# First norm over pairs of tiles, a shorter 1/rms, modulation in pairs and a split FFN buffer in a two-block transformer kernel

## The chip, the cores and the metric

The kernel runs on one core of one Trainium2 chip. The metric is the device time of one execution in microseconds (us), and lower is better. The engines are named as the profile names them: PE (TensorE, with PEld for its weight loads), DVE (VectorE), ACT (ScalarE), POOL (GpSimd) and SP (SyncE, which here only issues DMAs). SPq and ACTq are rows of DMA issue.

## What is computed

Two transformer blocks follow each other on 512 tokens of width 1024, in fp32. The first is an adaptive-norm block: six shifts, scales and gates come from a condition vector, the mixer is a gated linear attention (GLA) in both directions beside a differential attention over context and tokens, and a SwiGLU FFN follows. The second block has a mixer of windowed pooling and forgetting attention, a cross-attention to 256 memory rows, and an FFN with a width-3 convolution.

```python
def rmsnorm(x, g):  return x * rsqrt(mean(x * x, -1) + EPS) * g
def modulate(x, g, shift, scale):  return rmsnorm(x, g) * (1 + scale) + shift

# first block
sh1, sc1, gt1, sh2, sc2, gt2 = split(silu(c) @ w_mod + b_mod, 6)
px = modulate(x, norm1_g, sh1, sc1) @ w_in           # the context goes the same way: pc
mix = concat([gla_merge(og, r, gla_norm_g), diff_merge(od, diff_norm_g)]) @ w_out
x = x + gt1 * mix
x = x + gt2 * swiglu(modulate(x, norm2_g, sh2, sc2), w_ffn_in, w_ffn_out)
# second block
x = x + rms_norm(merged @ w_mix_out, mix_post_g)
x = x + rms_norm(mem_attention(rms_norm(x, xa_pre_g), rms_norm(mem, mem_g), w_xq, w_xkv, w_xo), xa_post_g)
x = x + rms_norm(conv_ffn(rms_norm(x, ffn_pre_g), w_up, conv_w, conv_b, w_down), ffn_post_g)
```

## The kernel before

**Layout and products.** Activations are held feature-major: eight tiles (KT = 8) of 128 features by 512 tokens (S = 512). Each weight matrix comes from HBM as fp32, in pieces of 512 KB mostly, into a ring of two buffers (tag `wf`), and `wsplit` (L171) cuts each into a high part, cast on ACT (L185), and the low rest, subtracted on DVE or POOL (L186). `mm3` makes each product of three matmuls: high x high, high x low, low x high (L194 to L196, and L283 to L285 where the tokens stand in the rows). PSUM has named slots: `acc`, `s` (from `s1` and `s2`), `mis`, `sums`.

**Order.** The engines' programs are laid out ahead by a scheduler that takes instructions by priority, and each engine then runs its own in order. `tc.issue_after(ins)` keeps an instruction behind another one. SP issues the loads in program order, and a load whose buffer isn't free holds those behind it.

**The start** (L401 to L500). X comes in four loads of two tiles. `normed_x` (L424) squares each tile, the even ones on ACT and the odd ones on DVE, and `sum_sq` (L308) sums over the features by matmuls with a column block of ones, four for a tile. `warm` (L481) issues matmuls on the identity whose results nobody reads: `WU` of them ahead of the first sum, `WX` ahead of each later one, `WW` behind the first modulations. `mod_tiles` and `mod_block` (L342) make the first 16 of 48 modulation tiles, from eight 1 MB loads (`wm`): matmuls with `silc` = silu(c) (L350), a copy out of PSUM (`mr`, L353), and `mod_sums` (L359): transposes (L362), a reduce over the partial sums (L363), the addition of the bias (L365).

**1/rms.** `rsqrt` (L156) makes v = mean + eps (DVE, L162), y = exp(-0.5 ln v) on ACT (L163, L164), and one Newton step in four DVE operations (L165 to L168). The names of its tiles say which norm it is: r_x and r_c (tokens and context in block one), r_n (second norm), r_post and r_pre (the norms of block two). `bcast` (L325) spreads r over the partitions with matmuls (L329).

**The other 32 modulation tiles** come in 32 steps of 512 KB. `mod_step` (L750) loads one piece into the same ring as the weights and runs its matmuls (L762); four steps fill one 512-wide `acc`, which ACT copies to `mr` (L766); `mod_end` (L769) calls `mod_sums` with a slot `s`. Two steps run in each of the first twelve of the 16 GLA units (`MU`, L1023), and `mod_end` in every second unit. The last eight steps are fillers of the attention stage.

**Fillers.** A list of jobs whose matmuls are laid into stages that don't fill PE; `fill_in` and `fill_to` take from it. In the attention stage they are, in order: the remaining gate projections (`gr_jobs`), `mix_in`, eight `mem_in` (load of a memory tile on ACT's queue, split by ACT and DVE, L1162 to L1165), the eight modulation steps, and the memory's keys and values (`mem_k`, `mem_v`). `mem_sq` (L714) squares the memory tiles early, through loads on ACT's queue.

**The output projection and the second norm.** `fm` (L217) runs a product tile by tile; after each quarter of a tile (`every`) it takes one step of whatever generator lies in `between`. `ev_out` (L1296) adds an output tile to X and squares it for the norm; `norm2` (L1304) yields `W4` or `W5` times, makes the statistics, yields, broadcasts and normalises. It is run for the two token halves; the second half's steps lie inside the first products of the FFN.

**The two FFNs** share `ffn_hidden` (L1330). It opens 22 hidden tiles in high and low parts: eight lie in free slots, the rest in the tiles `early`, `Fhi` and `Flo` of the pool that is passed (`fp` or `fp2`). Until the hidden state fills them, parts of `Fhi` and `Flo` take split weights (`room`). The second FFN's pool `fp2` (L1750) is opened when the pools of the cross-attention, `xp` and `xt` (L1658), have been closed (`xa.close`, L1742); it lies in their place. `KV` is the first tile of `xp`, and the last thing done with it is X = X + KV (L1428) of the second token half. In `fp2` stand, in order of allocation, `zl`, `early`, `Fhi`, `Flo`, and then the two buffers of `z`, which POOL first writes with a memset (L1760).

**The end.** `result` (L1789) sums the last squares, runs `rsqrt`, broadcasts (L1800), scales, adds and stores.

## Time and profile before

| | us |
|---|---|
| median of three runs | 1653.22 |
| lowest and highest | 1652.99, 1656.14 |
| the profiled execution | 1654.39 |
| its span, first to last instruction | 1652.6 |
| PE busy in it | 1600.5 (97%) |
| DVE, ACT, POOL busy | 948.7 (57%), 716.8 (43%), 214.1 (13%) |
| mean granted clock of PE | 0.989 |

Busy times are of one execution. A matmul's end is modelled, so a busy PE isn't always PE at its peak, and the rows of neighbouring instructions overlap a little. In a timeline the bracket behind a row tells how long the engine had been idle before it and what released it. The profiled execution's time is its span and 1.8 us around it.

### The profile page before, as it was taken

Reading aid. Unit: us, or ns where it says so; the run is one execution under the profiler, and the core shown is the slowest. Engines: PE = TensorE matmul, PEld = TensorE weight load, DVE = VectorE, ACT = ScalarE, POOL = GpSimd, SP = SyncE. Lnnn points to the kernel's source line nnn. Section 1 sums busy time; section 2 is a strip of 40 time slices with the busy share of each in tenths; the row PEclk is TensorE's granted clock in tenths of the full one; section 3 lists DMA queues with packets and bytes.
Section 4 is the critical chain, followed back from the end, with each engine's and each line's share of the span. In section 5 each row is a group of like instructions: output and inputs, shape, how many; then the busy total and the mean of one; then the engine's idle time right before and its main releaser. Section 6 shows DMA issues by size and latency. Waiting matters only on the chain.

```text
span 1652.6 us, 25497 instructions
## 1 busy us (share of the span) xinstructions
PE 1600.5 (97%) x10146; PEld 1359.2 (82%) x10146; DVE 948.7 (57%) x1799; ACT 716.8 (43%) x1345; POOL 214.1 (13%) x236
## 2 busy tenths in 40 slices
PE   8998999999999999999999999999998999999997
PEld 6898877768999888888889777888988988888887
DVE  5647787868756222223335676445788777776333
ACT  3534445567745323232223565224466544444221
POOL 0400000111012222110004000122000222221001
PEclk9999999999999999999999999999999999999998
DMA  9132245232323333332332212234210223323332
GB/s 373 53 95 81 79 152 160 80 122 74 130 72 109 90 91 101 102 91 89 101 117 71 77 39 64 90 102 146 86 50 27 90 90 102 102 90 96 96 93 74
DMA packets 48903, 162.98 MB, mean 99 GB/s; under 512 B 5648, under 2 KB 11280, under 8 KB 47248
## 3 DMA queue, kind: packets, MB, share of 16 engines
q1 hardware_dynamic: 45040, 157.74, 30.5%
q10 hardware_dynamic: 3456, 3.33, 0.7%
q8 instruction: 80, 1.31, 0.3%
q0 software_dynamic: 288, 0.28, 0.1%
q14 instruction: 39, 0.32, 0.1%
HBM read 158.46 MB, written 3.15 MB: 98 GB/s over the span
## 4 chain that ended last, share of the span: by engine, by line
PE 87%; DVE 6%; ACT 3%; issue 2%; DMA 1%; POOL 1%; ACTq 0%; DVEq 0%; POOLq 0%
PE acc L194 16%; PE acc L195 16%; PE acc L196 16%; PE s L195 5%; PE s L196 5%; PE s L194 5%; PE acc L284 3%; PE acc L283 2%; PE acc L285 2%; PE mis L1135 2%; PE mis L1607 1%; PE acc L762 1%; DVE wlo L186 1%; DMA wm<-in_w_mod 1%; PE s L1106 1%
## 5 line engine op out<-in xcount | busy, mean ns | idle before, releaser
L185 ACT CAST whi<-wf 128x1024 fp32r<-128x1024 f32 (+4 forms) x221 | 228.7, 1035 | 421.1 <-PE acc L195 291.0
L186 DVE TENSOR_TENSOR wlo<-wf,whi 128x1024 fp32r<-128x1024 f32 (+2 forms) x183 | 221.7, 1211 | 176.2 <-ACT whi L185 170.8
L195 PE MATMUL acc<-qlo,whi 128*128 128x512 f32 (+1 forms) x640 | 238.9, 373 | 0.0
L196 PE MATMUL acc<-qhi,wlo 128*128 128x512 f32 (+1 forms) x640 | 238.9, 374 | 0.0
L194 PE MATMUL acc<-qhi,whi 128*128 128x512 f32 (+1 forms) x640 | 238.6, 373 | 0.0
L194 PEld LDWEIGHTS acc<-qhi,whi 128*128 128x128 f32 x640 | 120.7, 189 | 19.7
L195 PEld LDWEIGHTS acc<-qlo,whi 128*128 128x128 f32 x640 | 120.6, 189 | 19.6 <-issue 0.2
L196 PEld LDWEIGHTS acc<-qhi,wlo 128*128 128x128 f32 x640 | 120.7, 189 | 19.4
L195 PE MATMUL s<-qlo,whi 128*128 128x512 f32 (+1 forms) x336 | 127.4, 379 | 0.0
L194 PE MATMUL s<-qhi,whi 128*128 128x512 f32 (+1 forms) x336 | 127.4, 379 | 0.0
L196 PE MATMUL s<-qhi,wlo 128*128 128x512 f32 (+1 forms) x336 | 127.4, 379 | 0.0
L186 POOL TENSOR_TENSOR wlo<-wf,whi 128x1024 fp32r<-128x1024 f32 x38 | 90.9, 2393 | 213.5 <-ACT whi L185 213.5
L1392 DVE TENSOR_TENSOR e<-e,s 128x512 f32<-128x512 f32 (+1 forms) x22 | 14.3, 652 | 154.0 <-PE s L196 153.8
L195 PE MATMUL acc<-glo,whi 128*128 128x512 f32 (+1 forms) x208 | 74.5, 358 | 0.1
L196 PE MATMUL acc<-ghi,wlo 128*128 128x512 f32 (+1 forms) x208 | 74.2, 357 | 0.0
L194 PE MATMUL acc<-ghi,whi 128*128 128x512 f32 (+1 forms) x208 | 74.2, 357 | 0.0
L194 PEld LDWEIGHTS s<-qhi,whi 128*128 128x128 f32 x336 | 63.2, 188 | 11.9
L196 PEld LDWEIGHTS s<-qhi,wlo 128*128 128x128 f32 x336 | 63.2, 188 | 11.9
L195 PEld LDWEIGHTS s<-qlo,whi 128*128 128x128 f32 x336 | 63.2, 188 | 11.6
L194 PE MATMUL acc<-Fhi,whi 128*128 128x512 f32 (+1 forms) x187 | 71.5, 383 | 0.0
L196 PE MATMUL acc<-Fhi,wlo 128*128 128x512 f32 (+1 forms) x187 | 71.5, 383 | 0.0
L195 PE MATMUL acc<-Flo,whi 128*128 128x512 f32 (+1 forms) x187 | 71.5, 382 | 0.0
(648 smaller groups left out, 3832.0 us busy)
## 6 DMA issues: line engine op xcount, KB each, us to landing
wf<-in_w_ffn_in SPq DMA_DIRECT2D x44, 512.0 KB, 3.6
wf<-in_w_up SPq DMA_DIRECT2D x44, 512.0 KB, 3.5
wm<-in_w_mod SPq DMA_DIRECT2D x32, 512.0 KB, 4.1
wm<-in_w_mod SPq DMA_DIRECT2D x8, 1024.0 KB, 13.1
wf<-in_w_ffn_out SPq DMA_DIRECT2D x16, 512.0 KB, 3.6
wf<-in_w_g SPq DMA_DIRECT2D x16, 512.0 KB, 3.5
wf<-in_w_down SPq DMA_DIRECT2D x16, 512.0 KB, 3.5
wf<-in_w_dv SPq DMA_DIRECT2D x8, 512.0 KB, 4.2
```

The source lines that it names most:

```text
L185: A.copy(hi[:, :n], wf[:, :n])
L186: (lo_eng or V).tensor_tensor(lo[:, :n], wf[:, :n], f32(hi[:, :n]), ALU.subtract)
L194: T.matmul(o, lhi, rhi, start=start, stop=False)
L195: T.matmul(o, lhi, rlo, start=False, stop=False)
L196: ins = T.matmul(o, llo, rhi, start=False, stop=stop).ins
L283: T.matmul(o, bhi(k), whi, start=k == 0, stop=False)
L284: T.matmul(o, bhi(k), wlo, start=False, stop=False)
L285: T.matmul(o, blo(k), whi, start=False, stop=k == KT - 1)
L762: T.matmul(p[32 * j:32 * j + 32, 256 * h:256 * h + 256], silc[:, 4 * kc + j], wf[:, j * 256:(j + 1) * 256], start=kc == 0, stop=kc == 1, s ...
L1106: T.matmul(s_[:, n0:n1], QF[:, c, ts], KA[:, c, n0:n1], start=True, stop=False)
L1135: T.matmul(p[:, :128], aT[:, kt * 128:(kt + 1) * 128], v, start=kt == 0, stop=kt == NKT - 1)
L1607: T.matmul(pO[:, ts], vz[:, kt, hp_, 64 * e:64 * e + 128], pT[:, kt * 128:(kt + 1) * 128], start=kt + e == 0, stop=kt - t + e == 1, skip_g ...
```

## The change

It has seven parts.
- **First norm.** Tiles are squared in pairs, one on ACT and one on DVE, and DVE adds the two squares; `sum_sq` runs once a pair. `WU` goes from 12 to 15 and `WX` from 2 to 1. The load of `cols` (biases, gains) moves from ACT's queue to SP's, behind X. The first modulation tiles are tied behind the last sum.
- **1/rms.** Ln reads its source itself, with the scale and a bias tile `epsc`; v is still made, beside it. Three operations follow instead of four.
- **Modulation in pairs.** `mod_step` fills 256 columns in two steps, and `mod_end` handles two tiles, once in each GLA unit. In the attention stage a pair of steps with its end stands behind each of the last two gate projections and the first two `mem_k`, instead of four and four behind `mem_in`.
- **Memory squares.** Their loads wait for the last activation of the context's modulation.
- **Output projection.** The first evictions are issued first and their squares after them.
- **Second norm.** `W4` goes from 2 to 1, and three yields instead of one stand between statistics and broadcast in the second half.
- **FFN buffer.** The high part is split into `Fend` (four tiles, allocated first) and `Fhi`; `early` is allocated last of these, `zl` at its first use. `room` has three entries instead of five, of which six in all (three of them None) are drawn.

```diff
-WU, WX, WW = 12, 2, 5
+WU, WX, WW = 15, 1, 5
-W4, W5 = 2, 1
+W4, W5 = 1, 1
...
+    epsc = const.tile([128, 1], F32, name="epsc")
+    nc.gpsimd.memset(epsc, EPS)
...
+        A.activation(y, src, AF.Ln, scale=scale, bias=epsc)
         V.tensor_scalar(v, src, scale, EPS, ALU.mult, ALU.add)
-        A.activation(y, v, AF.Ln)
         last_rs[0] = A.activation(y, y, AF.Exp, scale=-0.5).ins
-        V.tensor_tensor(t, y, y, ALU.mult)
-        V.tensor_tensor(t, t, v, ALU.mult)
-        V.tensor_scalar(t, t, -0.5, 1.5, ALU.mult, ALU.add)
-        V.tensor_tensor(r, y, t, ALU.mult)
+        V.scalar_tensor_tensor(t, v, -0.5, y, ALU.mult, ALU.mult)
+        V.tensor_tensor(t, t, y, ALU.mult)
+        V.scalar_tensor_tensor(r, t, 1.5, y, ALU.add, ALU.mult)
...
-        nc.scalar.dma_start(cols, a["cols"])
+        nc.sync.dma_start(cols, a["cols"])
...
-            for k in range(KT):
-                t = st2.tile([128, S], F32, tag=f"sqt{k % 2}", name="sqt")
-                if k % 2:
-                    V.tensor_tensor(t, x[:, k], x[:, k], ALU.mult)
-                else:
-                    A.activation(t, x[:, k], AF.Square)
+            for k in range(0, KT, 2):
+                t, u = (st2.tile([128, S], F32, tag=f"sqt{j}", name="sqt") for j in range(2))
+                A.activation(t, x[:, k], AF.Square)
+                V.tensor_tensor(u, x[:, k + 1], x[:, k + 1], ALU.mult)
+                V.tensor_tensor(u, u, t, ALU.add)
                 with tc.issue_after(warm(WU if k == 0 else WX)):
-                    sum_sq(pt, t, k == 0, k == KT - 1)
+                    last_warm[0] = sum_sq(pt, u, k == 0, k == KT - 2)
+            yield
...
-        mod_tiles(8)
-        next(nx)
-        im = mod_tiles(0)
+        queued(last_warm[0], lambda: mod_tiles(8))
+        ins = next(nx)
+        im = queued(ins, lambda: mod_tiles(0))
+        with tc.issue_after(ins):
+            next(nx)
...
-        nc.scalar.dma_start(m, a["memT"][:, k])
+        with tc.issue_after(hi_at[0]):
+            nc.scalar.dma_start(m, a["memT"][:, k])
...
-        if h == 1 and kc == 1:
-            mr = mid2.tile([128, 512], F32, tag="mr", name="mr")
-            A.copy(mr, p)
+        if kc == 1:
+            mr = mid2.tile([128, 256], F32, tag="mr", name="mr")
+            A.copy(mr, p[:, :256])
...
-        n = mod_at[0] // 4 - 1
+        n = mod_at[0] // 2 - 1
...
-            mod_sums(16 + 4 * n, 4, mr, s2)
+            mod_sums(16 + 2 * n, 2, mr, s2)
...
-        if u % 2 == 0:
-            mod_end()
+        mod_end()
...
+    mods_left = [[(0.8, mod_step), (0.8, mod_step), (0.3, mod_end)] for _ in range(MU, 16)]
     for m in range(GR, 4):
...
         fillers.append(gr_jobs[m])
+        fillers += mods_here()
     fillers.append((0.0, mix_in))
     for k in range(KT):
         fillers.append((0.0, lambda k=k: mem_in(k)))
-    for n in range(MU // 2, 8):
-        fillers += [(0.8, mod_step) for _ in range(4)] + [(0.6, mod_end)]
     for m in range(4):
...
         fillers.append((1.45, lambda m=m: mem_k(m)))
+        fillers += mods_here()
...
         r = fm_stats(sp, sqs[:, x:y], "n2")
-        yield
+        for _ in range(3 if x else 1):
+            yield
         bcast(rb[:, x:y], r)
...
         for m, (p, _, _) in enumerate(parts):
-            ev_out(m, 0, S, p)
+            V.scalar_tensor_tensor(X[m], p, mods[:, 16 + m, 0:1], X[m], ALU.mult, ALU.add)
+        for m in range(len(parts)):
+            add_sq(X[m], m, 0, S)
...
-        early = fp.tile([128, NP, 2, S // 2], F32, tag="Fh2", name="early")
+        NT = FT - KT - NP
+        last = fp.tile([128, 4, S], F32R, name="Fend")
         rest = []
         for n in ("Fhi", "Flo"):
-            t = fp.tile([128, FT - KT - NP, S], F32R, name=n)
+            t = fp.tile([128, NT if rest else NT - 4, S], F32R, name=n)
...
+        F[0] += [last[:, k] for k in range(4)]
+        early = fp.tile([128, NP, 2, S // 2], F32, tag="Fh2", name="early")
+        room = [t[:, 2 * j:2 * j + 2].rearrange("p k s -> p (k s)") for t in rest for j in range(3)]
+        room = [None] * 3 + [(room[j], room[3 + j], None) for j in range(3)]
```

## Rows read from the trace of the kernel before

**Rows 1.** The page, busy times: engine, us (share of span), instructions.
```profile
PE 1600.5 (97%) x10146; PEld 1359.2 (82%) x10146; DVE 948.7 (57%) x1799; ACT 716.8 (43%) x1345; POOL 214.1 (13%) x236
```

**Rows 2.** Waits of PE over the span: total us, times, longest us.
```profile
PE acc L762 <- DMA wm<-in_w_mod: 4.4, 4, 1.8
...
PE mis L1800 <- DVE r_post L168: 1.6, 1, 1.6
PE acc L194 <- DVE X L1297: 1.5, 1, 1.5
...
PE mis L329 <- DVE r_n L168: 1.3, 1, 1.3
...
PE acc L194 <- ACT mhi L1164: 0.9, 1, 0.9
...
PE acc L283 <- ACT mr L766: 0.7, 1, 0.7
PE s L362 <- DVE t_og L167: 0.6, 1, 0.6
...
PE mis L329 <- DVE r_x L168: 0.5, 1, 0.5
...
PE mis L329 <- DVE r_c L168: 0.5, 1, 0.5
```

**Rows 3.** Busy time by stretch: length, engines (instructions), granted clock, DMA share, GB/s.
```profile
25.94:29.35 3.41, 3.41 (x12) 1.84 (x14) 3.41 (x6) 0.00 (x0) 0.00 (x0) 0.50 1.02 384
...
1278.63:1285.46 6.83, 6.22 (x27) 5.92 (x28) 6.07 (x12) 6.59 (x11) 2.03 (x4) 0.50 0.50 148
185.00:335.00 150.00, 139.06 (x1881) 108.83 (x1879) 123.62 (x290) 78.21 (x205) 8.98 (x18) 0.98 0.39 123
```

**Rows 4.** Timeline of the first norm, PE and DVE: start, us, what.
```profile
1.85 4.65 PE L485 MATMUL s<-ident 128*128 128x128 f32 x24 [1.85 <-POOL down L556]
6.34 0.98 PE L311 MATMUL mis<-ones,sqt 128*128 128x32 f32 x8
...
6.44 0.41 DVE L408 TENSOR_TENSOR silc<-cT,silc 128x256 f32<-128x256 f32 x1
...
8.70 0.69 DVE L430 TENSOR_TENSOR sqt<-X 128x512 f32<-128x512 f32 x1 [0.58 <-PE mis L311]
```

**Rows 5.** The first eight modulation loads (`wm`, 0 to 60 us): durations ns, starts.
```profile
L350 PE MATMUL acc<-wm,silc x128: 379/379/569, 16.6 to 48.6; 128*32 128x256 f32 x128
L399 SPq DMA_DIRECT2D wm<-in_w_mod x8: 328/426/737, 3.1 to 26.8; - x8
...
DMA to landing us min/median/max: 7.2/13.1/18.6
```

**Rows 6.** Timeline of the last 1/rms.
```profile
1641.91 0.48 DVE L1787 TENSOR_SCALAR Yd<-acc,cols 128x256 f32<-128x256 f32 x1 [0.93 <-ACT sqt L1786]
...
1642.60 0.16 DVE L162 TENSOR_SCALAR v_post<-mis 128x2 f32<-128x2 f32 x1 [0.20 <-PE mis L311]
1642.79 0.20 ACT L163 ACTIVATE y_post<-v_post 128x2 f32<-128x2 f32 x1 [0.92 <-DVE v_post L162]
1643.02 0.20 ACT L164 ACTIVATE y_post<-y_post 128x2 f32<-128x2 f32 x1
...
1644.16 1.19 PE L1800 MATMUL mis<-ident,r_post 128*128 128x128 f32 x4 [1.60 <-DVE r_post L168]
```

**Rows 7.** Timeline of the second norm's second half.
```profile
500.56 0.60 PE L311 MATMUL mis<-ones,sqs 128*128 128x32 f32 x4 [0.34 <-DVE sqs L1293]
...
504.96 1.23 DVE L186 TENSOR_TENSOR Flo<-wf,Fhi 128x1024 fp32r<-128x1024 f32 x1 [0.21 <-ACT Fhi L185]
```

**Rows 8.** Timeline at the opening of the second FFN: ACT, POOL, PE.
```profile
1277.68 1.05 ACT L185 CAST Fhi<-wf 128x1024 fp32r<-128x1024 f32 x1 [0.97 <-DVE X L1428]
...
1277.84 0.13 POOL L1760 MEMSET z<- 128x2 f32 x2 [131.07 <-DVE X L1428]
...
1278.78 0.58 PE L194 MATMUL s<-qhi,Fhi 128*128 128x256 f32 x1 [4.89 <-ACT Fhi L185]
```

More of the change, by code (lines that the diff above doesn't have):

```diff
@@ L33 @@
 NF = 2
+NWF = 2
 T0 = 1
@@ L173, in wsplit @@
         if wf is None:
-            wf = ring.tile([128, RW], F32, tag="wf", name="wf", bufs=2)
+            wf = ring.tile([128, RW], F32, tag="wf", name="wf", bufs=NWF)
         if shape is None:
@@ L310, in sum_sq @@
         for t in range(sq.shape[-1] // 128):
-            T.matmul(pt[:, 32 * t:32 * t + 32], sq[:, t * 128:(t + 1) * 128], ones, start=start and t == 0, stop=stop,
-                     skip_group_check=True)
+            ins = T.matmul(pt[:, 32 * t:32 * t + 32], sq[:, t * 128:(t + 1) * 128], ones, start=start and t == 0, stop=stop,
+                           skip_group_check=True).ins
+        return ins
     def fm_stats(pool, sq, name):
@@ L750, in mod_step @@
     def mod_step():
-        n, h, kc = mod_at[0] // 4, mod_at[0] // 2 % 2, mod_at[0] % 2
-        if n == 8:
+        n, kc = mod_at[0] // 2, mod_at[0] % 2
+        if n == 16:
             return
         mod_at[0] += 1
-        wf = ring.tile([128, RW], F32, tag="wf", name="wm", bufs=2)[:, :1024]
-        nc.sync.dma_start(wf, a["w_mod"][n, h, kc].rearrange("p k n -> p (k n)"))
-        if h == 0 and kc == 0:
+        wf = ring.tile([128, RW], F32, tag="wf", name="wm", bufs=NWF)[:, :1024]
+        nc.sync.dma_start(wf, a["w_mod"][n // 2, n % 2, kc].rearrange("p k n -> p (k n)"))
+        if kc == 0:
             mod_p["p"] = acc()
@@ L812 @@
     Rq = gp.tile([128, NLEV, 128], BF16, name="Rq")
-    lt0 = ring.tile([128, RW], F32, tag="wf", name="lt0", bufs=2)
+    lt0 = ring.tile([128, RW], F32, tag="wf", name="lt0", bufs=NWF)
     nc.sync.dma_start(lt0[:, :NLEV * 128], a["LT"])
     V.tensor_copy(LT, lt0[:, :NLEV * 128])
-    lt1 = ring.tile([128, RW], F32, tag="wf", name="lt1", bufs=2)
+    lt1 = ring.tile([128, RW], F32, tag="wf", name="lt1", bufs=NWF)
     nc.sync.dma_start(lt1[:, :512], a["Lsm"])
@@ L1220, in out_part, with xk_ahead, mods_here @@
                         lambda p, hi, lo: parts.append((p, hi, lo)), alloc=alloc)
+    def xk_ahead(m):
+        return 0.0, lambda: fm_ahead(a["w_xk"], "xk", m, ML & 1 and G)
+    mods_left = [[(0.8, mod_step), (0.8, mod_step), (0.3, mod_end)] for _ in range(MU, 16)]
+    def mods_here():
+        return mods_left.pop(0) if mods_left else []
     for m in range(GR, 4):
-        fillers += [gr_ahead(m + 1)] if m < 3 else [(0.0, lambda: fm_ahead(a["w_xk"], "xk", 0, ML & 1 and G))]
+        fillers += [gr_ahead(m + 1)] if m < 3 else [xk_ahead(0)]
         fillers.append(gr_jobs[m])
+        fillers += mods_here()
     fillers.append((0.0, mix_in))
@@ L1227 @@
         fillers.append((0.0, lambda k=k: mem_in(k)))
-    for n in range(MU // 2, 8):
-        fillers += [(0.8, mod_step) for _ in range(4)] + [(0.6, mod_end)]
     for m in range(4):
         if m < 3:
-            fillers.append((0.0, lambda m=m: fm_ahead(a["w_xk"], "xk", m + 1, ML & 1 and G)))
+            fillers.append(xk_ahead(m + 1))
         fillers.append((1.45, lambda m=m: mem_k(m)))
+        fillers += mods_here()
     fillers += [(1.45, lambda hf=hf, t=t: mem_v(hf, t)) for hf in range(2) for t in range(2)]
@@ L1332, in ffn_hidden @@
         F = [[sl[:, k] for k in range(KT)] for sl in slot]
-        early = fp.tile([128, NP, 2, S // 2], F32, tag="Fh2", name="early")
+        NT = FT - KT - NP
+        last = fp.tile([128, 4, S], F32R, name="Fend")
         rest = []
         for n in ("Fhi", "Flo"):
-            t = fp.tile([128, FT - KT - NP, S], F32R, name=n)
+            t = fp.tile([128, NT if rest else NT - 4, S], F32R, name=n)
             rest.append(t)
-            F[len(rest) - 1] += [t[:, k] for k in range(FT - KT - NP)]
-        room = [t[:, 2 * j:2 * j + 2].rearrange("p k s -> p (k s)") for t in rest for j in range(5)]
-        room = [None] * 3 + [(room[j], room[5 + j], None) for j in (2, 3, 4, 0, 1)]
+            F[len(rest) - 1] += [t[:, k] for k in range(t.shape[1])]
+        F[0] += [last[:, k] for k in range(4)]
+        early = fp.tile([128, NP, 2, S // 2], F32, tag="Fh2", name="early")
+        room = [t[:, 2 * j:2 * j + 2].rearrange("p k s -> p (k s)") for t in rest for j in range(3)]
+        room = [None] * 3 + [(room[j], room[3 + j], None) for j in range(3)]
         waits = []
@@ L1750 @@
     with tc.tile_pool(name="fp2", bufs=1) as fp:
-        zl = fp.tile([128, 2, 4, 2], F32, name="zl")
+        zl = []
         def pair2(pg_, pu_, i, x, y, held):
             ready(rb_of, x)
+            if not zl:
+                zl.append(fp.tile([128, 2, 4, 2], F32, name="zl"))
             res = []
@@ L1761, in pair2 @@
                 else:
[L1762 removed]
+                    G.tensor_copy(z[:, x:x + 2], zl[0][:, g, i])
                 V.tensor_tensor(z[:, 2 + x:2 + y], p, rb[:, x:y], ALU.mult)
                 if y < S:
[L1765 removed]
+                    G.tensor_copy(zl[0][:, g, i], z[:, y:y + 2])
                 t = fp.tile([128, S], F32, tag=f"zc{g}", name=f"zc{g}", bufs=1)[:, x:y] if held is None else held[:, g]
```

4 lines of the change are left out of this document (1 added, 3 removed).

## The prediction

> **What bounds the kernel now.** I began with the page: TensorE (PE) is busy for 97% of the span [rows 1], so 1652.6 - 1600.5 = 52.1 us of the span have no matmul, and an edit pays only where it shortens one of those holes, or a stretch in which PE's work is itself overhead. Next came the list of PE's waits [rows 2]: each row names what PE stood for, who released it, the total and the longest. The reader should see that it is a long list of short waits, and that the change touches all of the nine rows shown, if most of them little. Then I read the granted clock by stretch [rows 3]: 3.41 us at 0.50, the lower of the two levels (1.2 GHz against 2.4), follow some of these waits, and work at half clock takes twice as long, so such a stretch costs 3.41 / 2 = 1.7 us. Last, the timelines around each edit [rows 4, 6 to 8].
>
> **First norm in pairs.** Before, PE sets this stage: after 24 warm-up passes (12 matmuls of two) from 1.85 on, each of the eight tiles costs 0.98 us of sum passes and two warm-ups, from 6.34 to the first modulation matmul at 16.6 [rows 4, 5], (16.6 - 6.34) / 8 = 1.29 us a tile. DVE has slack: its third square waits 0.58 us for PE to give a tile back [rows 4]. After the change PE has half the sums (four rounds of 0.98) and one warm-up between them, and DVE has a square and an add a pair. An add of two 128x512 tiles isn't in this stage; I take it at the 0.69 of the multiply of the same shape. DVE's first square is over by 6.44. From there: one add 0.69, the condition's multiply 0.41 [rows 4], as much again for two small operations behind it, three pairs of 2 x 0.69 = 4.14: 12.1. Then one round of sums, 0.98: 13.0, against 16.6: **-3.6 us**. The longer first warm-up (30 passes at 4.65 / 24 = 0.19 us, until 7.7) ends about when the first add does, so it hides. The bounds: -4.3 if the seven operations overlap by 0.1 each, as the first square and the multiply behind it seem to; -2.5 if X or `cols` (now behind X on SP's queue) hold DVE for a microsecond.
> Does the gain survive? The loads don't move, so every use comes 3.6 us closer to its landing. PE's list has no wait of this stage's modulation matmuls (L350) for a load; the last of the eight 1 MB loads is issued at 26.8, landings take 7.2 to 18.6 us with a median of 13.1, and the last use is at 48.6 [rows 5]. By the median it lands at 39.9, by the maximum at 45.4; both are before 48.6 - 3.6 = 45.0 or at it. I keep the whole gain, and price its loss as a rival.
>
> **1/rms.** One chain is seen bare at the end [rows 6]: DVE's v starts at 1642.60, Ln at 1642.79, Exp ends at 1643.22, and PE goes on at 1644.16. The change lets Ln start in v's place (0.19 gained, v then lies beside Exp) and makes four DVE operations three: 1644.16 - 1643.22 = 0.94 for four and the hops, about 0.2 each. So -0.39 a chain. v has to come behind Ln, since two readers of one PSUM tile take turns here (L1787 is released by L1786, which only reads the same `acc` [rows 6]), but Exp's 0.20 covers it. PE waits for r_x, r_c, r_n and the last r_post [rows 2]: r_x, r_c and r_post get 0.39 each, r_n is counted below. Three chains before and in the second FFN lie in a row of DVE work, where only the operation saved counts: 3 x 0.2. Sum 3 x 0.39 + 0.6 = **-1.8** (-1.0 with r_x, r_c and r_post alone, each a little short; -2.4 if the other three count in full).
>
> **Modulation in pairs, GLA stage.** Loads, matmuls and the load buffers (`NWF` is 2, as before) stay. Each unit now ends a pair: two copies of 256 columns stand for one of 512, and a turn of the `s` slot with its transposes, reduce and add per unit where it was per two. The slot `acc` comes free after two steps instead of four; PE waits 0.7 us once for that copy [rows 2] and would mostly not, -0.7. Against it stand six more turns of `s`; the one wait on such a turn is 0.6 us [rows 2], once in six. DVE is 123.62 / 150 = 82% busy here [rows 3], so its small extra operations can delay others. I take **-0.7**, the nearest row; bounds -3 (a clock dip goes too) and +4 (each new turn waits 0.6).
>
> **Modulation in the attention stage.** The last eight steps stood in one block behind the memory inputs; now pairs follow the gates and the first two `mem_k`. PE waited 4.4 us in four pieces for these weight loads, the longest, 1.8, in this stage [rows 2]. Spread out, a load has other work to land beside. But the same steps were what PE had to do while ACT split the memory tiles, and PE waits 0.9 for that split already [rows 2]. I take half of the longest wait, **-0.9**; bounds -1.8 - 1.7 = -3.5 with a half-clock stretch gone too, and +2.7 if three more waits of 0.9 come.
>
> **Norm 2, second half.** The statistics come one step earlier, the broadcast keeps its place three steps behind. Now PE waits 0.34 for the squares and 1.3 for r_n, whose last operation queued behind a 1.23-us weight split at 504.96 [rows 2, 7]. A shorter chain passes ahead of that split: -1.3. The squares are no earlier, though: a step is 12 matmuls of 0.12 us, so the 0.34 can become 0.34 + 1.44 = 1.8; I take a third of that, +0.5. **-0.8** (-1.6 to +1.5).
>
> **Small ones.** Evictions of `w_out` before the squares: PE waits 1.5 us for the third eviction [rows 2], which stands behind a weight split on DVE that stays; -0.2 (0 to -1.5). The memory squares' loads leave ACT's queue in the first stage: -0.2 (0 to -0.4).
>
> **FFN buffer in two tiles.** Here is the largest wait, 4.89 us, and 6.83 us at half clock behind it [rows 2, 3, 8]. The split puts a tile where KV was, so that the weight cast (`Fhi`) needn't wait for KV's last reader, X L1428. But rows 8 show that not only ACT's `Fhi` is released by that X: GpSimd's memset of `z`, after 131 us of idleness, is too, 0.16 us later, and `z` is allocated behind Fhi and Flo, far from KV. What all share is not an address but the pool `fp2`, opened when the pools of cross-attention close. If the wait is on the pool, cutting a tile in two changes nothing: **0** (down to -8, below).
>
> **Sum.** -3.6 - 1.8 - 0.7 - 0.9 - 0.8 - 0.4 + 0 = -8.2 us. Against the profiled execution's 1654.39 (span 1652.6 and 1.8 around it) that is 1646.2. The median of the runs shown, 1653.22, lies 1.2 below that execution: 1645.0, which I predict.
>
> **Rivals.**
> A, the buffer's wait is per tile: `Fhi` starts as soon as its load is there, PE keeps most of the 4.89 us and half of the 6.83 at half clock (3.4). DVE's chain to the new X still has to end before PE can be fed for long, so I count -4 to -8: 1645.0 - 6 = 1639. For it: the tile is laid exactly over KV. Against it: the row of `z`.
> B, the start's gain is given back at the next waits. The half-clock stretch at 25.94 to 29.35 [rows 3] follows waits of PE on the first hidden state; with a quicker start the same producers have to keep up with less slack, and one more such dip (1.7) and as much again in the waits that draw it take 3.4 back: 1645.0 + 3.4 = 1648.4. The Trainium skill ("TensorE: Matmul & The Clock Gate", section "HAM oscillation — how this bites in real kernels") says that a PE that keeps stopping for its operands falls to the lower clock again and again; by that rule the warm-ups taken out here cost such a dip in the first stage itself. PE's new rounds (0.98 + 2 x 0.19 of 1.38) leave almost no gap, so I don't put it into the sum.
> S, slower: in the GLA stage every unit takes the `s` slot. Place: twelve units between 185 and 335. Price: the wait on such a turn, 0.6, in each of twelve units is 7.2; three dips of 1.7 that such waits draw are 5.1; together +12.3: 1645.0 + 12.3 = 1657.3. It decides once the stage loses more than 8.2 + 3.3 = 11.5 us, about 1 us a unit. For it: DVE at 82%. Against it: six such turns before cost one wait.
> That the change doesn't do what it says is, for the buffer, my forecast itself.
>
> **Chances.** About 3.3 us (0.2%) is what a measurement of this kernel can tell from no change: faster means below 1649.9, slower above 1656.5. Forecast 0.57 (0.50 of it faster, 0.07 same), A 0.15, all faster, B 0.17 (0.08 faster, 0.09 same), S 0.11, slower. So faster 0.73, same 0.16, slower 0.11. The range takes in A, the forecast's bounds as far as they don't all fall together, and B, and ends below S: 1636 to 1655.
>
> **What would show it.** First modulation matmul at 12.5 to 14 instead of 16.6, and L350 still with no wait for a load. In the last chain, v beside Exp, three DVE operations, PE's wait at 1.2 instead of 1.6. In GLA, L362 with no waits beyond 0.6 and the half-clock stretches no more than before. No wait of 1.3 on r_n, and one of at most 1.8 on the squares. Before the second FFN, `Fhi` and `z` still released together by X L1428, with a hole near 4.5. The prediction is wrong if `Fhi` starts clearly ahead of that X (A), if the gain at 17 us is gone by 50 (B), or if the GLA stage is longer than before (S).

## The result and the profile after

The changed kernel takes 1644.26 us (median of four runs, 1643.65 to 1646.13) against 1653.11 for the kernel before (four runs): a ratio of 0.9946 with a 95% interval of 0.9929 to 0.9963. The profiled execution took 1646.13, its span is 1644.2. The predicted 1645.0 is as good as met, but not by the terms that I had added up. The span is 8.4 us shorter, and a table of stages shows where. A stage ends where PE starts a certain row: the first product on the hidden state (`s<-hhi`), the context's product that waits for the q/k norm, the first row on `ghc` (GLA begins), the first on `sgt` (attention begins), the first on `kh` (w_out), the sums of squares of norm 2's second half, the last row on `xh`, the last broadcast of r_post. Each length is the difference of two such starts in the timelines, in us.

| kernel | to hidden state | to q/k norm | to GLA | GLA | attention | to norm 2 | to last w_xo | second FFN | end | span |
|---|---|---|---|---|---|---|---|---|---|---|
| before | 22.99 | 101.82 | 18.19 | 178.58 | 144.38 | 34.59 | 763.76 | 380.61 | 7.69 | 1652.6 |
| after | 24.45 | 100.50 | 21.63 | 174.88 | 137.69 | 34.69 | 763.65 | 379.04 | 7.68 | 1644.2 |
| `cols_act` | 21.28 | 99.85 | 20.89 | 175.89 | 138.11 | 34.69 | 763.78 | 378.20 | 7.62 | 1640.3 |
| `cols_wx3` | 19.25 | 99.99 | 23.03 | 176.66 | 137.83 | 34.67 | 763.97 | 378.98 | 8.04 | 1642.4 |
| `first_old` | 23.47 | 104.63 | 22.76 | 177.07 | 140.49 | 34.69 | 763.70 | 379.03 | 7.91 | 1653.8 |
| `rsqrt_old` | 22.72 | 100.42 | 18.18 | 177.68 | 139.98 | 35.19 | 766.44 | 379.26 | 7.54 | 1647.4 |
| `rsqrt_only` | 23.17 | 104.41 | 22.64 | 178.05 | 142.74 | 34.69 | 761.66 | 378.06 | 7.78 | 1653.2 |
| `cols_qk` | 20.89 | 98.73 | 18.07 | 176.76 | 137.90 | 34.68 | 763.56 | 379.02 | 7.92 | 1637.5 |
| `mods_old` | 22.68 | 100.54 | 21.22 | 179.00 | 141.48 | 35.76 | 766.59 | 378.22 | 7.53 | 1653.0 |
| `att_block` | 25.55 | 100.54 | 20.87 | 174.86 | 144.48 | 35.09 | 762.36 | 378.13 | 7.53 | 1649.4 |
| `n2_old` | 20.91 | 101.67 | 21.09 | 177.14 | 137.96 | 34.69 | 763.12 | 379.07 | 7.69 | 1643.3 |
| `ffn_old` | 21.04 | 100.47 | 21.00 | 175.35 | 138.17 | 34.69 | 763.58 | 378.66 | 7.69 | 1640.7 |
| `room_g` | 24.28 | 100.50 | 21.11 | 173.04 | 138.03 | 34.68 | 763.60 | 371.65 | 7.68 | 1634.6 |
| `best` | 23.12 | 98.72 | 18.07 | 176.78 | 137.95 | 34.85 | 763.05 | 371.26 | 7.69 | 1631.5 |

Each line is one profiled execution, and the same code doesn't give the same line. The start, unchanged from "after" in five of the kernels, ends anywhere from 20.9 to 25.6 us; GLA, in the eight that share its code, takes 173.0 to 177.1. Much of this is where the half-clock stretches fall. The second table gives, for three stages, the time at granted clock 0.50 (the lower of the two levels, 1.2 GHz) and an estimate of the length at full clock: the length less half of that time, as if PE worked all through it (sixteen modulation matmuls take 1.94 us at 0.50 in the changed kernel and 1.07 at 1.00 in `cols_wx3`; both rows are below).

| kernel | start: at 0.50 | less half | GLA: at 0.50 | less half | attention: at 0.50 | less half |
|---|---|---|---|---|---|---|
| before | 0 | 23.0 | 6.83 | 175.2 | 10.24 | 139.3 |
| after | 10.24 | 19.3 | 6.83 | 171.5 | 0 | 137.7 |
| `cols_act` | 3.41 | 19.6 | 6.83 | 172.5 | 0 | 138.1 |
| `cols_wx3` | 0 | 19.3 | 10.24 | 171.5 | 0 | 137.8 |
| `first_old` | 0 | 23.5 | 6.83 | 173.7 | 6.83 | 137.1 |
| `rsqrt_old` | 6.83 | 19.3 | 10.24 | 172.6 | 3.41 | 138.3 |
| `rsqrt_only` | 0 | 23.2 | 6.83 | 174.6 | 6.83 | 139.3 |
| `cols_qk` | 3.41 | 19.2 | 10.24 | 171.6 | 0 | 137.9 |
| `mods_old` | 6.83 | 19.3 | 10.24 | 173.9 | 3.41 | 139.8 |
| `att_block` | 10.24 | 20.4 | 6.83 | 171.4 | 10.24 | 139.4 |
| `n2_old` | 3.41 | 19.2 | 10.24 | 172.0 | 0 | 138.0 |
| `ffn_old` | 3.41 | 19.3 | 6.83 | 171.9 | 0 | 138.2 |
| `room_g` | 10.24 | 19.2 | 3.41 | 171.3 | 0 | 138.0 |
| `best` | 6.83 | 19.7 | 10.24 | 171.7 | 0 | 137.9 |

Below I build only on differences that are larger than this spread, or that several kernels repeat.

The start got no shorter. DVE's and PE's timelines of the changed kernel (line numbers are those of each kernel):

```profile
10.10 0.15 DVE L1164 TENSOR_SCALAR gd<-cols 128x1 f32<-128x1 f32 x1 [1.51 <-DMA cols<-in_cols]
10.18 1.29 DVE L433 TENSOR_TENSOR sqt<-X 128x512 f32<-128x512 f32 x2
...
12.13 1.92 PE L313 MATMUL mis<-ones,sqt 128*128 128x32 f32 x8 [1.50 <-DVE sqt L434]
...
16.11 1.94 PE L353 MATMUL acc<-wm,silc 128*32 128x256 f32 x16
```

A column of gains for a much later norm (`gd`) stands in DVE's program between the squares. It needs `cols`, which now comes behind X. DVE stands 1.51 us, the last two pairs are late, PE stands 1.50, and the granted clock, from within that wait on, is 0.50 for 10.24 us, as the busy time by stretch shows (the clock is the third figure from the end):

```profile
11.39:21.63 10.24, 9.50 (x56) 7.32 (x60) 2.92 (x11) 1.43 (x4) 0.00 (x0) 0.50 1.02 410
130.85:134.27 3.42, 3.10 (x14) 3.13 (x15) 1.69 (x5) 1.04 (x3) 0.00 (x0) 0.50 0.15 38
...
1270.90:1277.73 6.83, 6.09 (x27) 5.79 (x28) 6.07 (x12) 6.62 (x11) 2.16 (x5) 0.50 0.49 143
```

The first modulation matmul comes at 16.11 instead of 16.6 [rows 5], and the hidden state's first product 1.5 us later than before. The half-clock time alone accounts for that: less half of it the start takes 19.3 us, as it does, within 0.4, in ten of the eleven kernels with pairs (20.4 in `att_block`), against 23.0 to 23.5 in the three without.

A new loss stands between the q/k norm and GLA (18.19 to 21.63 us). ACT's timeline there and PE's next wait, first before, then after:

```profile
122.51 0.33 ACTq L717 DMA_DIRECT2D mk<-in_memT  x1
124.78 0.22 ACT L163 ACTIVATE y_qk<-v_qk 128x24 f32<-128x24 f32 x1 [2.03 <-DVE v_qk L162]
...
126.36 0.42 ACT L719 ACTIVATE mks<-mk 128x256 f32<-128x256 f32 x1 [1.10 <-DMA mk<-in_memT]
...
129.06 0.36 PE L283 MATMUL acc<-whi,hhi 128*128 128x256 f32 x1 [1.14 <-ACT qsq L645]
```

```profile
122.45 0.37 ACT L650 ACTIVATE qsq<-acc 128x256 f32<-128x256 f32 x1
124.18 0.31 ACT L165 ACTIVATE y_qk<-qss,epsc 128x24 f32<-128x24 f32 x1 [1.36 <-DVE qss L651]
124.24 0.33 ACTq L723 DMA_DIRECT2D mk<-in_memT  x1
...
129.49 0.42 ACT L725 ACTIVATE mks<-mk 128x256 f32<-128x256 f32 x1 [4.65 <-DMA mk<-in_memT]
...
131.17 0.55 PE L285 MATMUL acc<-whi,hhi 128*128 128x256 f32 x1 [3.12 <-DVE kdv L654]
```

Ln no longer stands behind v but at the head of ACT's program, waiting for the sums. The issue of a memory tile's load is queued behind it and comes 1.7 us later (124.24 for 122.51), and ACT goes on 5.25 us after the issue instead of 3.85; why the load takes longer is not shown. ACT stands 4.65 us for it, and with ACT the copies and squares that free PSUM for PE, which then works at half clock for 3.42 us (the second stretch above).

The gains are in the two stages with modulations. PE's waits there (total us, times, longest), first from 146 to 321.6 us, before and after:

```profile
PE acc L762 <- DMA wm<-in_w_mod: 2.6, 3, 1.1
...
PE s L977 <- DVE E L965: 1.3, 2, 1.0
...
PE mis L1007 <- DVE AT L999: 0.4, 1, 0.4
```

```profile
PE s L983 <- DVE E L971: 4.7, 6, 1.9
PE mis L1013 <- DVE AT L1005: 2.5, 3, 1.8
...
PE acc L768 <- DMA wm<-in_w_mod: 0.2, 1, 0.2
```

Then from 321 to 460 us, before and after:

```profile
PE acc L762 <- DMA wm<-in_w_mod: 1.8, 1, 1.8
PE acc L195 <- DVE mlo L1165: 0.9, 1, 0.9
PE acc L194 <- ACT mhi L1164: 0.9, 1, 0.9
```

```profile
PE acc L196 <- ACT whi L187: 1.3, 1, 1.3
...
PE acc L196 <- ACT mhi L1169: 0.4, 1, 0.4
```

The 4.4 us for modulation loads and the 0.9 for the memory split [rows 2] are down to 0.2 and 0.4. In GLA the waits for two of DVE's own tiles, `E` and `AT`, rose from 1.7 to 7.2 us, against the gain; they are 4.9 us in `rsqrt_old`, without the new 1/rms, and 6.2 in `rsqrt_only`, with nothing else changed, so neither part alone explains it; why is not shown. The attention stage's mean clock is up as well. First before, the two half-clock stretches in the stage and the whole of it, then the stage after:

```profile
360.44:363.86 3.42, 3.42 (x14) 2.56 (x14) 0.56 (x4) 1.38 (x3) 0.00 (x0) 0.50 0.35 126
374.10:380.93 6.83, 6.31 (x32) 5.92 (x31) 3.99 (x9) 3.96 (x10) 0.68 (x2) 0.50 0.29 96
...
321.59:465.96 144.37, 137.00 (x924) 114.57 (x925) 107.14 (x223) 97.39 (x220) 16.69 (x30) 0.96 0.33 105
```

```profile
321.45:459.15 137.70, 133.79 (x928) 111.36 (x928) 108.28 (x224) 98.62 (x223) 15.19 (x30) 1.00 0.34 111
```

PE's idle time fell from 7.4 to 3.9 us and its busy time, for the same products, from 137.0 to 133.8. Of the 6.7 us of the stage, 5.1 go with the half-clock time by the estimate above.

In the second norm a wait moved (PE's timeline; [rows 7] are the same place before):

```profile
493.84 0.60 PE L313 MATMUL mis<-ones,sqs 128*128 128x32 f32 x4 [1.75 <-DVE sqs L1305]
...
498.66 0.60 PE L332 MATMUL mis<-ident,r_n 128*128 128x128 f32 x4
```

Before the second FFN all is as it was [rows 8], ACT, POOL and PE in turn:

```profile
1270.08 1.05 ACT L187 CAST Fhi<-wf 128x1024 fp32r<-128x1024 f32 x1 [0.97 <-DVE X L1446]
...
1270.24 0.13 POOL L1780 MEMSET z<- 128x2 f32 x2 [128.63 <-DVE X L1446]
...
1271.18 0.58 PE L196 MATMUL s<-qhi,Fhi 128*128 128x256 f32 x1 [4.50 <-ACT Fhi L187]
```

### The profile page after: what moved, and what is told of

It is laid out like the page before. It is cut to its first block, busy times and chain, and to the rows that moved or that the text cites. A ratio compares the mean times of both kernels' runs of the same rounds, so it can differ in the third digit from the quotient of the medians.

```text
span 1644.2 us, 25457 instructions
## 1 busy us (share of the span) xinstructions
PE 1595.5 (97%) x10098; PEld 1357.4 (83%) x10098; DVE 948.9 (58%) x1791; ACT 720.3 (44%) x1353; POOL 211.5 (13%) x237
## 4 chain that ended last, share of the span: by engine, by line
PE 86%; DVE 6%; ACT 3%; DMA 2%; issue 2%; POOL 1%; SPq 0%; ACTq 0%; DVEq 0%; POOLq 0%
PE acc L197 16%; PE acc L196 16%; PE acc L198 16%; PE s L198 5%; PE s L196 5%; PE s L197 5%; PE acc L285 3%; PE acc L286 3%; PE acc L287 2%; PE mis L1140 1%; PE mis L1625 1%; PE acc L768 1%; DMA mk<-in_memT 1%; DVE QX L970 1%; PE s L1111 1%
## 5 line engine op out<-in xcount | busy, mean ns | idle before, releaser
L197 PEld LDWEIGHTS acc<-qlo,whi 128*128 128x128 f32 x640 | 120.9, 189 | 19.6 <-issue 0.2
L198 PEld LDWEIGHTS acc<-qhi,wlo 128*128 128x128 f32 x640 | 120.8, 189 | 19.6
L285 PE MATMUL acc<-whi,hhi 128*128 128x256 f32 (+1 forms) x224 | 66.8, 298 | 3.3 <-DVE kdv L654 3.1
L287 PE MATMUL acc<-whi,hlo 128*128 128x256 f32 (+1 forms) x224 | 65.1, 291 | 0.0
```

Of the source, the lines that this page charges most:

```text
L197: T.matmul(o, lhi, rlo, start=False, stop=False)
L198: ins = T.matmul(o, llo, rhi, start=False, stop=stop).ins
L285: T.matmul(o, bhi(k), whi, start=k == 0, stop=False)
L287: T.matmul(o, blo(k), whi, start=False, stop=k == KT - 1)
```

## The experiments

The theory after the result: the start is held by `cols` and the clock; the new 1/rms costs at the q/k norm what it doesn't elsewhere; the place of the modulation steps makes the gain; the FFN's wait is on the pool. The rival in general: the total came from the start and the chains after all, and stages only shifted. Ratios are against the kernel before in the same series; for the changed kernel it is 0.9946 (0.9929 to 0.9963). The kernel before itself has a median of 1653.11 in the changed kernel's series and of 1655.14 to 1656.67 in the others, so I compare kernels by their ratios; 0.001 is 1.7 us.

### The start: `cols_act`, `cols_wx3`, `first_old`

```diff
-        nc.sync.dma_start(cols, a["cols"])
+        nc.scalar.dma_start(cols, a["cols"])
```

> The changed kernel with one line undone: cols is loaded through ACT's queue again, not through SP's behind X. Theory: in the changed kernel DVE stands 1.51 us at 8.6 to 10.1 for cols, the squares behind it are late, PE waits 1.50 and works at half clock for 10.24 us. Without that the last sum ends near 13 (16.1 in the changed kernel), the half-clock stretch is gone, the first product on the hidden state starts at 20 to 21 instead of 24.45, and if the gain lasts the time is some 3.5 us below the changed kernel's 1644.3: about 1641. Rival: the start is quicker, but what follows is bound by loads or by DVE, the lead is used up by 125 us and the time is 1644 to 1645.

Measured: 1642.64 us, ratio 0.9917 (0.9904 to 0.9929). DVE doesn't stand for `cols`; it does, for 1.0 to 1.5 us, in all seven kernels with that load behind X, and in none of the four with it on ACT's queue. PE's timeline:

```profile
11.81 1.08 PE L313 MATMUL mis<-ones,sqt 128*128 128x32 f32 x8 [1.08 <-DVE sqt L434]
...
14.05 1.93 PE L353 MATMUL acc<-wm,silc 128*32 128x256 f32 x16
```

The sums end at 14.05 instead of 16.11 and the stage at 21.28, but not at 13: PE still has a hole of 1.08 us, and half-clock stretches of 3.41 us stand at 13.75 and 23.99. This is no shorter than `n2_old` and `ffn_old` come out, which have the load behind X and DVE's wait (20.9 and 21.0), so the shorter start is not shown to be the load's doing: the end of the start goes with the half-clock time, 20.9 to 21.3 us with 3.41, 22.7 to 23.1 with 6.83 and 24.3 to 25.6 with 10.24. The whole is 1.6 us faster by the medians and 4.8 by the ratios, whose intervals just touch.

```diff
-WU, WX, WW = 15, 1, 5
+WU, WX, WW = 15, 3, 5
```

> The changed kernel with cols on ACT's queue and three warm-ups instead of one ahead of each later sum. Theory: with one warm-up PE has holes of 0.3 to 1.1 us between the rounds of sums, and the half-clock stretches in the first 27 us come from these; with three it has none, the clock stays at 1.00 there and the first product on the hidden state starts at 19.5 to 20.5 (21.3 with cols alone): time 1641 to 1642. Rival: the warm-ups delay the sums by as much as the clock gives; 21 to 22, time 1642.6 or more.

With three warm-ups a round, on top of `cols_act`:

```profile
13.13 1.07 PE L353 MATMUL acc<-wm,silc 128*32 128x256 f32 x16
...
19.25 0.50 PE L196 MATMUL s<-hhi,whi 128*128 128x512 f32 x1 [0.86 <-ACT hhi L381]
```

The stage ends at 19.25: 22.99 - 19.25 = 3.7 us, what the prediction had promised. The clock stays at 1.00 until 22.31. The lead of 2.0 us on `cols_act` is still 1.9 at the q/k norm (119.24 against 121.13 us) and gone where GLA begins (142.27 against 142.02). It goes in the wait behind Ln, which is longer here, and in a longer half-clock stretch behind it. PE's wait and the stretch in `cols_wx3`, then in `cols_act`:

```profile
125.66 0.55 PE L285 MATMUL acc<-whi,hhi 128*128 128x256 f32 x1 [3.33 <-ACT qsq L650]
...
124.71:131.54 6.83, 5.88 (x27) 5.91 (x28) 2.22 (x7) 1.57 (x4) 0.00 (x0) 0.50 0.08 19
```

```profile
126.55 0.55 PE L285 MATMUL acc<-whi,hhi 128*128 128x256 f32 x1 [2.33 <-ACT qsq L650]
...
126.39:129.80 3.41, 3.25 (x15) 3.28 (x16) 1.43 (x5) 0.57 (x2) 0.00 (x0) 0.50 0.15 42
```

The time is 1644.86, ratio 0.9924 (0.9913 to 0.9936), which can't be told from `cols_act`. So the start's arithmetic was right for an undisturbed start, and the new Ln at the q/k norm took the lead back. With v ahead of Ln there (`cols_qk` below) a lead on the kernel before of 5.2 us at the q/k norm is 5.3 at GLA; the two edits together were not tried.

`first_old` puts the first norm, its warm-ups and the order around it back as before (the diff's parts for `WU`, `cols`, `normed_x` and `mod_tiles`, reversed).

> The changed kernel with the first norm, its warm-ups and cols as before. Theory: with cols behind X the pairs win nothing, since DVE's wait and the half clock take what PE's fewer sums give: first product on the hidden state at 22.5 to 23 (20 to 25.5 in the runs with the pairs and cols on SP), time 1643.5 to 1645.5. Rival: the pairs are worth their 3.6 us even so; the time is 1647 or more.

Measured: 1652.32 us, ratio 0.9976 (0.9964 to 0.9988), 5 us slower than the changed kernel by the ratios; the rival's time came, but not for its reason. The stage to the hidden state (23.47) is no worse than the changed kernel's 24.45, which has 10.24 us at half clock. The loss comes later (4.1 us before the q/k norm, 1.1 behind it, 2.2 in GLA, 2.8 in attention; the profiled execution is the slowest of nine, which took 1645.60 to 1655.91), and first at 64 us, on ACT and PE:

```profile
60.76 0.59 ACT L381 ACTIVATE hc<-cX,mods,scc 128x256 fp32r<-128x256 f32 x1
61.25 1.09 ACT L187 CAST whi<-wf 128x1088 fp32r<-128x1088 f32 x1
...
66.81 0.39 PE L286 MATMUL acc<-wlo,hhi 128*128 128x272 f32 x1 [2.77 <-DVE wlo L188]
```

A weight's cast stands behind the eight activations of the context (`hc`) instead of ahead of them, and PE waits 2.77 us. The engines' order is laid out ahead, and an edit in the first 20 us turned it at 60. `rsqrt_only` below has the same turned order without any edit of the first norm, so the order is not the pairs' own doing. What the pairs' saving at the start is worth to the end is therefore not shown by this run.

### 1/rms: `rsqrt_old`, `rsqrt_only`, `cols_qk`

```diff
-        A.activation(y, src, AF.Ln, scale=scale, bias=epsc)
         V.tensor_scalar(v, src, scale, EPS, ALU.mult, ALU.add)
+        A.activation(y, v, AF.Ln)
         last_rs[0] = A.activation(y, y, AF.Exp, scale=-0.5).ins
-        V.scalar_tensor_tensor(t, v, -0.5, y, ALU.mult, ALU.mult)
-        V.tensor_tensor(t, t, y, ALU.mult)
-        V.scalar_tensor_tensor(r, t, 1.5, y, ALU.add, ALU.mult)
+        V.tensor_tensor(t, y, y, ALU.mult)
+        V.tensor_tensor(t, t, v, ALU.mult)
+        V.tensor_scalar(t, t, -0.5, 1.5, ALU.mult, ALU.add)
+        V.tensor_tensor(r, y, t, ALU.mult)
```

> The changed kernel with the old 1/rms (Ln reads v, four DVE operations). Theory: Ln of the q/k norm at 124 us reads its sums itself, so it waits at the head of ACT's queue and holds the load of a memory tile behind it (issued 124.24 instead of 122.51); with the old form that load goes out before Ln, ACT's wait of 4.65 us for it falls to about 1.1, PE's wait at 128 from 3.1 to 1.1, and the half-clock stretch at 131 goes: 2 to 3.5 us won there. Against it the bare chains get 0.3 to 0.4 us longer each: at the end, at r_x and r_c, and r_n's wait may come back (1.3). In all 1643 to 1645.5. Rival: the edit has no such cost; the wait at 128 stays at 3.1 us and the time rises by 1.8 to 3 us, to 1646 or 1647.

Measured: 1650.71 us, ratio 0.9972 (0.9960 to 0.9984). ACT's timeline at the q/k norm:

```profile
123.11 0.22 ACT L166 ACTIVATE y_qk<-v_qk 128x24 f32<-128x24 f32 x1 [1.95 <-DVE v_qk L165]
...
126.85 0.42 ACT L726 ACTIVATE mks<-mk 128x256 f32<-128x256 f32 x1 [2.00 <-DMA mk<-in_memT]
```

ACT waits 2.0 us for the tile instead of 4.65, PE's wait is 1.15 and the stage 18.18, as before the change: the cost of 3.4 us is shown. It stands in all ten kernels with the new Ln at the q/k norm (20.87 to 23.03 us) and in none of the four with v ahead of it (18.07 to 18.19). The sum that I expected did not come: GLA, attention, norm 2 and the stretch to the last w_xo are 2.8, 2.3, 0.5 and 2.8 longer than in the changed kernel, and the old form is slower by 4.3 us (0.9972 against 0.9946, with intervals that overlap). Some 1.7 us in each of the three large ones is longer half-clock time (a stretch of 6.83 us follows norm 2), and the rest, 0.6 to 1.2, is about what kernels with the same code differ by. So where the saved DVE operation pays is not shown.

The kernel before with the new form alone (the same edit from the other side):

> The kernel before with the new 1/rms alone. Theory: as in the changed kernel it costs 2 to 3 us from the q/k norm to the first product of GLA (40.1 becomes 42 to 43.5) and gains in the loaded stages: 1 to 3 in GLA (178.6), 2 to 3 in attention (144.4), 1 to 2 from the second norm on, 0.4 at the end: 2 to 5 us less, 1648 to 1651. Rival: its gain in the changed kernel needs the modulation in pairs; alone it moves the time by less than 1 us.

Measured: 1654.83 us, ratio 0.9991 (0.9983 to 1.0000): 1.5 us, between 0 and 2.8. It loses 2.6 us before the q/k norm, by the same turned order as `first_old` (PE waits 2.78 us for that split), and 4.4 after it, and wins 0.5 in GLA, 1.6 in attention (half-clock time alone: 139.3 us in both without it), 2.1 in the stretch to the last w_xo and 2.6 in the second FFN. The rival holds for the total: alone the edit is worth next to nothing.

`cols_qk` keeps the three operations and lets Ln read v, as before, in the q/k norms only, with `cols` on ACT's queue:

```diff
+        if name == "qk":
+            V.tensor_scalar(v, src, scale, EPS, ALU.mult, ALU.add)
+            A.activation(y, v, AF.Ln)
+        else:
             A.activation(y, src, AF.Ln, scale=scale, bias=epsc)
             V.tensor_scalar(v, src, scale, EPS, ALU.mult, ALU.add)
```

> The changed kernel with cols on ACT's queue (as in the run of that name) and with Ln reading v, as before, in the q/k norms alone; the three DVE operations stay everywhere. Theory: the new Ln costs only where it waits at the head of ACT's queue with a load's issue behind it, that is at the q/k norm at 120 us; with v ahead of it there, the stretch from that norm's wait to the first product of GLA (ghc, L862) falls from 23.9 to about 21 us, and the rest stays as with cols alone (1642.6): 1639 to 1640.5. Rival: the stretch is short only with the old form as a whole, because DVE's order changes with it; then it stays at 23 to 24 us and the time at 1642.6.

Measured: 1641.03 us, ratio 0.9919 (0.9903 to 0.9934). The stage falls from the 20.89 us of `cols_act` to 18.07, by 2.8 where 2.9 were expected. Its total can't be told from `cols_act` by the ratios; by the medians it is 1.6 us ahead.

### Modulation: `mods_old`, `att_block`

`mods_old` undoes all of the modulation's part. `att_block` keeps the pairs and undoes their place in the attention stage:

```diff
-        fillers += mods_here()
     fillers.append((0.0, mix_in))
     for k in range(KT):
         fillers.append((0.0, lambda k=k: mem_in(k)))
+    for n in range(MU, 16):
+        fillers += [(0.8, mod_step), (0.8, mod_step), (0.3, mod_end)]
...
         fillers.append((1.45, lambda m=m: mem_k(m)))
-        fillers += mods_here()
```

> The changed kernel with the old modulation (512 columns a tile, four steps; the last eight steps in one block behind the memory inputs). Theory: most of the gain is in these two stages; from 150 to 321 us it comes back by 3 to 4 us, from 321 to 458 by 6 to 7, so 1653 to 1655. Rival: the two stages got shorter because other edits shifted their phase against loads and clock; then at most 4 us come back and the time is 1645 to 1648.

> The changed kernel with pairs kept, but the last eight modulation steps in one block behind the memory inputs again, as before. Theory: the place of the steps makes the gain of the attention stage: it is 6 to 7 us longer, GLA (150 to 321 us) is as in the changed kernel, the time 1650 to 1651. Rival: the smaller tile (acc held for two steps, not four) makes it: at most 2 us come back, 1644 to 1646.

Measured: `mods_old` 1653.10 us, ratio 0.9982 (0.9971 to 0.9992); `att_block` 1654.56, ratio 0.9992 (0.9983 to 1.0001). Against 0.9946 these are 6 and 7.6 us. With the block back, attention is 144.48 us, the length of before, in the fastest of twelve executions; GLA keeps its 174.86. PE's waits in `att_block` from 321 to 460 us:

```profile
PE mis L1071 <- issue: 2.3, 1, 2.3
PE s L365 <- ACT mr L772: 1.9, 1, 1.9
PE acc L768 <- DMA wm<-in_w_mod: 1.9, 1, 1.9
PE acc L768 <- DVE rs L743: 1.2, 1, 1.2
```

So the place of the steps makes the gain of this stage: with the block it takes 141.5 to 144.5 us in four kernels, with the steps spread out 137.7 to 138.2 in eight, and 140.0 and 140.5 in `rsqrt_old` and `first_old`. Most of it is the clock: the four have 3.41 to 10.24 us at 0.50, the eight none and the other two 3.41 and 6.83. Less half of that, it is 139.3 to 139.8 against 137.1 to 138.3. In GLA the same estimate gives the pairs some 1.4 to 3.3 us: 173.9 in `mods_old` and 174.6 with the new 1/rms alone, against 171.3 to 172.5 with both (173.7 in `first_old`); without the new 1/rms it is 175.2 before and 172.6 in `rsqrt_old`. In `mods_old` PE again waits three times for a modulation load there, 0.7 to 1.1 us each. That the slot held for four steps, over two units, delays the loads behind it is the likely reason; it wasn't tried apart.

### Norm 2: `n2_old`

```diff
-W4, W5 = 1, 1
+W4, W5 = 2, 1
...
-        for _ in range(3 if x else 1):
-            yield
+        yield
```

> The changed kernel with the old steps of the second norm (statistics two steps behind, one step to the broadcast). Theory: the earlier statistics only move a wait: PE now stands 1.75 us for the squares; with the old steps it stands 0.3 to 0.6 for them and, since the shorter 1/rms passes ahead of the weight split, 0 to 0.5 for r_n: 1 to 1.5 us less, about 1643. Rival: r_n's wait of 1.3 us comes back and the time stays at 1644.3.

Measured: 1645.33 us, ratio 0.9938 (0.9924 to 0.9953), no difference that can be told. PE waits 0.29 for the squares and 0.66 for r_n; the changed kernel waits 1.75 and nothing. So the rival holds for the time, and r_n's wait came back by half:

```profile
493.45 0.60 PE L313 MATMUL mis<-ones,sqs 128*128 128x32 f32 x4 [0.29 <-DVE sqs L1305]
...
497.18 0.68 PE L332 MATMUL mis<-ident,r_n 128*128 128x128 f32 x4 [0.66 <-DVE r_n L170]
```

### The second FFN: `ffn_old`, `room_g`, and `best`

`ffn_old` has the buffer of before. `room_g` gives two of the six early weights room outside the new pool, in tiles whose last readers are matmuls:

```diff
+        for j in (0, 1):
+            room[3 + j] = tuple(t[:, 4 + 2 * j:6 + 2 * j].rearrange("p k s -> p (k s)") for t in slot) + (None,)
```

> The changed kernel with the old buffer (Fhi in one tile, early and zl first). Theory: the wait is on the pool and not on a tile, so nothing moves: PE's hole before the second FFN 4.5 us, Fhi and z released by the same X, time within 1 us of the changed kernel's 1644.3. Rival: the split is worth something after all, the hole is back at 4.9 or more and the time 1645.5 or above.

> The changed kernel, but in ffn_hidden the fourth and fifth split weights go into the upper halves of the two tiles for the first eight hidden tiles (tags hhi and hlo, whose last readers are matmuls that end before 1267), and only the sixth into Fhi and Flo. Theory: what holds PE for 4.50 us before the second FFN is the first write into the new pool fp2; a weight outside it can be split as soon as PE is done with w_xo, so the hole falls to 1 to 3 us, and the 6.83 us at half clock behind it get shorter or go: 2 to 6 us less, 1638.5 to 1642.5. DVE has two splits of 1.2 us more in its busiest stretch, which may give 1 to 2 us back. Rival: PE waits there for DVE's chain to the new X and for the z that free its slots; the hole moves to the next slot and the time stays at 1644.

Measured: `ffn_old` 1643.07 us, ratio 0.9929 (0.9915 to 0.9944), with the same wait of 4.50 us: the split is worth nothing that can be told. `room_g` takes 1636.24 us, ratio 0.9885 (0.9868 to 0.9902). Its ACT timeline, and the busy time by stretch across the place of the hole:

```profile
1269.77 1.05 ACT L187 CAST Fhi<-wf 128x1024 fp32r<-128x1024 f32 x1 [0.97 <-DVE X L1448]
```

```profile
1262.00:1282.00 20.00, 19.76 (x166) 19.58 (x166) 19.62 (x42) 15.88 (x30) 4.38 (x14) 1.00 0.12 42
```

`Fhi` is released by the same X as ever, but PE no longer asks for it then: the hole is gone, the clock stays at 1.00, and the second FFN is 379.0 - 371.65 = 7.4 us shorter. Only the place of the weight changed; so the wait is on the pool, and its full price was the hole and the half clock behind it, 4.5 + 6.83 / 2 = 7.9.

`best` joins `cols_qk`, `room_g` and `n2_old`.

> The changed kernel with four edits of the earlier runs together: cols on ACT's queue, Ln behind v in the q/k norms, two split weights of each FFN in the tiles of the first hidden tiles, the old steps of the second norm. Theory: the gains lie in separate stages and add: 1644.3 - 3 (start and q/k norm) - 7.4 (second FFN) - 0.5 = about 1632 to 1634. Rival: each gain is partly a phase of the clock, and together they give less than 8: 1636 or more.

Measured: 1633.95 us (1631.67 to 1635.12), ratio 0.9861 (0.9847 to 0.9875): 10 us below the changed kernel and 22 below the one before by the medians, 14 and 23 by the ratios. The rival falls, and the gains add: by the ratios `room_g` alone is 10.1 us ahead of the changed kernel and `cols_qk` 4.5.

## Why the prediction came out

The total was met by luck, because errors of both signs cancelled: the stages changed by +1.5 us to the hidden state, -1.3 to the q/k norm, +3.4 to GLA, -3.7 in GLA, -6.7 in attention and -1.6 in the second FFN, and by 0.1 or less elsewhere.

- **First norm, -3.6: measured +1.5 at the hidden state.** The step that failed is in rival B: "leave almost no gap, so I don't put it into the sum". PE's rounds did leave gaps, and 10.24 us at half clock put 5.1 us on top. The sum of DVE operations itself was right: -3.7 in `cols_wx3`, whose start has no half-clock time, and -3.7 in the changed kernel less half of it (23.0 to 19.3). The wait for `cols`, which I bounded by a microsecond and 1.1 us of price, came with 1.51 us but doesn't decide, since the starts with it and without it are equally long but for the clock. The Trainium skill ("TensorE: Matmul & The Clock Gate", "HAM oscillation — how this bites in real kernels") tells of a PE that falls to the lower clock again and again because it keeps stopping for its operands, there for longer and for loads. The trace agrees with it for shorter holes: 10.24 us at 0.50 in the changed kernel, and none in this stage with three warm-ups a round. The step "I keep the whole gain" held to the q/k norm, where `cols_wx3` is 5.6 us ahead of the kernel before, and failed there, not for the modulation loads that I had looked at: 0.7 are left at GLA. The 1.3 us won ahead of the q/k norm go with the stretch of 3.41 us at 25.94 [rows 3], worth 1.7, which doesn't come in the changed kernel; rival B expected one more.
- **1/rms, -1.8: measured -4.3 in the changed kernel, -1.5 alone.** A bare chain behaves as worked out: v stands behind Ln and beside Exp, PE's last wait is 1.29 (predicted 1.2). What was missed is that Ln took a wait onto ACT, with the issue of a load behind it: 3.4 us at the q/k norm. I had asked who waits behind v on DVE, and not what is queued behind Ln on ACT. What outweighs that loss in the changed kernel lies in several stages and is in good part half-clock time; its cause stays open.
- **GLA, -0.7: measured -3.7; attention, -0.9: measured -6.7.** The mechanism was the one named (loads that land beside other work); the terms were mis-sized. Attention is beyond my bound of -3.5; GLA is beyond its -3 in this execution, and its own spread is as large. In attention I priced one wait where the block of steps stands in a crowd of six (0.5 to 1.8 us each, between 357 and 376), and one half-clock stretch of 1.7 where two, of 3.41 and 6.83 us, fall among them. The fear that the memory split would starve PE was wrong: its waits fell with the others. Rival S did not come: no transpose into the `s` slot (L365) waits over 0.5 us.
- **Norm 2, -0.8: measured +0.1.** r_n's wait went as worked out (-1.3). The squares' wait became 1.75, the 1.8 of the bound; the step that failed is the third of it that I took.
- **Small ones, -0.4: not shown.** Neither was tried apart. At the first product of `w_out` PE waited 1.5 us for the eviction [rows 2] and waits 1.3 for a weight's cast in the changed kernel.
- **FFN buffer, 0: measured 0** (4.89 to 4.50 by the shorter chains ahead of it: it is 4.9 in `rsqrt_old` and 4.5 in `rsqrt_only`). The reading of the memset's row was right and is now shown by `room_g`; rival A fell.
